# Late layer norms of the feed-forward stage: one step per gate and up block, several tiles under way, ln1 rows loaded once

## The chip, the cores and the metric

The kernel runs on one core of a Trainium2 chip. Its time is the device time of one execution in microseconds (us). The core has a matrix engine (PE in the profile, TensorE), three engines for elementwise work (DVE is VectorE, ACT is ScalarE, POOL is GpSimd) and a queue engine, SP, that here only issues DMAs. ACT also issues DMAs, for stores. Each engine works through its own instructions in order, and waits for the others by semaphores.

## The reference, cut to what matters

One layer of a network over 2048 latent tokens of width 1024: a mixer (attention beside a state-space branch, with a gated unit), then a feed-forward stage. The change lies at the seam of the two:

```python
x = layer_norm(DN_ALPHA * x + g1 * y_lat, lp['ln1_g'], lp['ln1_b'])
x = layer_norm(DN_ALPHA * x + g2 * swiglu(modulate(x, sh2, sc2), lp['w_gate_up'], lp['w_down']),
               lp['ln2_g'], lp['ln2_b'])

def modulate(x, shift, scale):
    return layer_norm(x) * (1 + scale) + shift
def swiglu(u, w_gate_up, w_down):
    gate, up = jnp.split(u @ w_gate_up, 2, axis=-1)
    return (jax.nn.silu(gate) * up) @ w_down
```

So between the mixer and the feed-forward each token passes two layer norms: one with the rows ln1_g and ln1_b (its result, x1, is also needed at the very end), one without, followed by shift and scale.

## The kernel before

All large products are fp32 in three passes: each operand is split into a high and a low part, and `mm3` (L63 to L65) multiplies high by high, low by high, high by low. A high part is a copy of the operand in fp32r (L53, on POOL for weights), a low part the difference (L58, mostly on DVE). So a weight tile that PE multiplies first passes POOL, then DVE.

The feed-forward class works on the tokens in two halves of 1024 (b = 0, 1), and in each on 22 blocks of 128 gate and 128 up columns (f = 0 to 21). A block is a 2 x 2 Strassen-Winograd scheme: seven products (0 to 6) of 12 matmuls, 84 in all, into the PSUM banks pa, pb, pc and pd (`block`). `weights(f + 1)` loads the next block's four weight pieces (tile wraw) and forms and splits their seven combinations (w0 to w3 and three g tiles) while block f is multiplied. Within a block DVE combines the banks: L1676, L1683, L1685, L1687, L1691. L1685 reads bank c, and product 6 goes on adding onto the same bank: PE can't begin product 6 (rows `pc<-oh,gh`) before DVE has done L1685. Product 0 of a block shows as `pa<-oh,w0h`.

The norms of the first 1024 tokens are done before the stage. Those of the second 1024 ("late" tiles 0 to 7, of 128 tokens each, held in n_scr) are done by `late(i)` beside the blocks of b = 0. The late tile i is started once every two blocks, all of it but the transposes at once: load n_scr and the four half rows of ln1_g and ln1_b (L1708, 256 KB each), norm (statistics L1714 and L1716 on DVE, square root and scale on ACT, L73 and L1721, and a few one-column operations on DVE between them), multiply and add the rows on POOL (L1727, L1728), store x1 (L1729, on ACT's queue), copy on DVE (L1732), norm again. Two blocks later the tile is transposed on PE (L1738, 8 transposes), shifted and scaled by ACT (L1741) and stored to u2_scr (L1743), from where `tokens(1)` loads it before b = 1. The tiles live in the pool ff_u (name uraw), 8 buffers; a tile's start takes eight of them (r, ln1_g, ln1_b, u2, two halves each).

No order is written out for this stage: the framework's scheduler lines up each engine's instructions by the order of the program text and its own estimates, so a change in the text shifts rows on every engine, also in the stages ahead.

Of the kernel before, what the change touches and what calls it, by code (L numbers as in the profile page):

```python
# [1541 lines left out]
class FeedForward:  # L1542
# [48 lines left out]
    def tokens(self, b):  # L1591

        nc, V = self.nc, self.nc.vector
        u = {n: [] for _, _, n in PRODUCTS}
        for k in range(4):
            t = {PRODUCTS[i][2]: self.pair() for i in STEP}
            r = {n: self.up.tile([128, 512], F32, name="uraw", bufs=8) for n in ("B11", "B12", "B21", "B22", "T1")}
            for n in ("B11", "B12", "B21", "B22"):
                j, h = int(n[1]) - 1, int(n[2]) - 1
                row, col = (j * 4 + k) * 128, (b * 2 + h) * 512  # L1600
                nc.sync.dma_start(r[n], self.E.u2_scr[row:row + 128, col:col + 512])

# [19 lines left out]
        return u  # L1622
# [34 lines left out]
    def block(self, b, f, w, u):  # L1657
# [35 lines left out]
        V.tensor_tensor(c22, c22, u2, ALU.mult)  # L1693
        self.store(b, f, 1, c22)

    def late(self, i):

        nc, E = self.nc, self.E
        V, P = nc.vector, nc.gpsimd
        t = NLAT // 128 - LATE + i  # L1700

        def piece():
            return self.up.tile([128, 512], F32, name="uraw", bufs=8)

        def load(src):
            p = [piece(), piece()]
            for h in range(2):
                nc.sync.dma_start(p[h], src(slice(h * 512, (h + 1) * 512)))  # L1708
            return p

        def norm(r):
            st = self.sm.tile([128, 2, 6], F32, name="lst", tag="lst", bufs=2)
            for h in range(2):
                V.bn_stats(st[:, h], r[h])  # L1714
            mv = self.sm.tile([128, 2], F32, name="bmv", tag="bmv")
            V.bn_aggr(mv, st)  # L1716
            rs = rsqrt(nc, self.sm, mv[:, 1:2], E.eps)
            nb = self.sm.tile([128, 1], F32, name="nb", tag="nb")
            V.tensor_scalar(nb, mv[:, 0:1], rs, -1.0, ALU.mult, ALU.mult)
            for h in range(2):  # L1720
                nc.scalar.activation(r[h], r[h], AF.Identity, bias=nb, scale=rs)  # L1721

        r = load(lambda h: E.n_scr[i, :, h])
        lg, lb = [load(lambda h: E.I[n][0:1, h].broadcast_to([128, 512])) for n in ("ln1_g", "ln1_b")]
        norm(r)
        for h in range(2):
            P.tensor_tensor(r[h], r[h], lg[h], ALU.mult)  # L1727
            P.tensor_tensor(r[h], r[h], lb[h], ALU.add)  # L1728
            nc.scalar.dma_start(E.x1_scr[t * 128:(t + 1) * 128, h * 512:(h + 1) * 512], r[h])  # L1729
        u2 = [piece(), piece()]  # L1730
        for h in range(2):
            V.tensor_copy(u2[h], r[h])  # L1732
        norm(u2)
        yield
        for h in range(2):
            pt = self.ps.tile([128, 512], F32, name="pd")
# [9 lines left out]
    def hidden(self, q, f):  # L1746

        t = self.pair()
        raw = self.up.tile([128, 512], F32, name="uraw", bufs=8)
# [62 lines left out]
    def run(self):  # L1812
        tc, nc, E, I = self.tc, self.nc, self.E, self.I
        with ExitStack() as st:
            self.tp = st.enter_context(tc.tile_pool(name="ff_t", bufs=8, side="right", reuse_waits="tile"))
            self.op = [st.enter_context(tc.tile_pool(name="ff_o%d" % k, bufs=7, side="right", reuse_waits="tile"))
                       for k in (3, 2, 1, 0)][::-1]
            self.up = st.enter_context(tc.tile_pool(name="ff_u", bufs=8, side="right", reuse_waits="tile"))
            self.rows = st.enter_context(tc.tile_pool(name="ff_r", bufs=1, reuse_waits="tile"))
            self.sm = st.enter_context(tc.tile_pool(name="ff_s", bufs=4, reuse_waits="tile"))  # L1820
            self.ps = st.enter_context(tc.tile_pool(name="ff_p", bufs=2, space=PSUM, reuse_waits="tile"))
            w = self.weights(0)
            u = self.tokens(0)
            late = iter(())
            for b in range(2):
                if b:
                    u = self.tokens(b)
                for f in range(NFB):
                    nxt = self.weights((f + 1) % NFB) if b == 0 or f + 1 < NFB else None
                    (self.block if b or f else self.first)(b, f, w, u)  # L1830
                    w = nxt
                    if b == 0 and f % 2:
                        next(late, None)
                        late = self.late(f // 2 - 1) if 0 <= f // 2 - 1 < LATE else iter(())
                        next(late, None)
            self.g2 = row_bcast(nc, self.rows, E.mod_scr[3:4, :], "g2b")
            self.lg = row_bcast(nc, self.rows, I["ln2_g"], "l2g")
            self.lb = row_bcast(nc, self.rows, I["ln2_b"], "l2b")
# [154 lines left out]
```

## Time and profile before

| | |
|---|---|
| median of 3 runs (lowest to highest) | 3283.35 us (3279.94 to 3284.1) |
| the profiled execution's own time | 3283.37 us |
| its span in the profile | 3281.6 us |
| PE busy | 3076.4 us, 94% of the span |
| DVE, POOL, ACT busy | 69%, 48%, 39% |
| gate and up blocks of b = 0 | about 1879 to 2350 us in the span |

The profiled execution lies 0.02 us from the median, so sums made against it hold for the runs as they are; 1.8 us of its time lie outside the span. A busy share is an average over the whole span; what an engine waits for is read in the stage in question.

### The profile page before, as it was taken

The numbers are of one execution on the slowest core, as the hardware profiler recorded it, in microseconds if no ns is written. First come the engines' busy times: TensorE is split into PE (matmuls) and PEld (weight loads), VectorE is DVE, ScalarE is ACT, GpSimd is POOL, SyncE is SP. The second block draws the span as 40 slices with busy tenths as digits, with TensorE's granted clock in tenths as the row PEclk, the third lists the DMA queues.
The fourth block names the chain that finished last, engine by engine and source line by source line (L and its number), as shares of the span: only waits on it lengthen the run. The fifth ranks groups of instructions, "written<-read, shape, count | busy, mean of one in ns | idle before, by whom it ended". The sixth has DMA issues, their size and how long they took to land. (4 is left out here: it accounts for less than half of the span.)

```text
span 3281.6 us, 48246 instructions
## 1 busy us (share of the span) xinstructions
PE 3076.4 (94%) x16693; PEld 2615.6 (80%) x16693; DVE 2272.8 (69%) x3938; ACT 1279.9 (39%) x2404; POOL 1581.2 (48%) x2365
## 2 busy tenths in 40 slices
PE   7899998999999999999789889889899999999998
PEld 4788877988988988888667677668688888888886
DVE  7755465888888776788477686666766666566667
ACT  2333354777777666667434233222201002112110
POOL 3755333877877899834243242332322222243444
PEclk9999999999999999999999999999899999999999
DMA  7444474111110222211768543343422224655544
GB/s 235 159 155 133 150 241 131 31 26 29 33 30 23 63 70 80 85 58 32 206 163 215 176 139 116 116 126 96 135 87 90 78 84 133 201 184 165 189 149 137
DMA packets 376885, 389.49 MB, mean 119 GB/s; under 512 B 97656, under 2 KB 270776, under 8 KB 376640
## 3 DMA queue, kind: packets, MB, share of 16 engines
q1 hardware_dynamic: 306640, 314.65, 32.3%
q10 hardware_dynamic: 70000, 71.75, 6.4%
q8 instruction: 132, 2.16, 0.3%
q14 instruction: 113, 0.93, 0.1%
HBM read 281.82 MB, written 104.48 MB: 118 GB/s over the span
## 5 line engine op out<-in xcount | busy, mean ns | idle before, releaser
L1033 DVE TENSOR_TENSOR ptl<-tps,pth 128x512 fp32r<-128x512 f32 x576 | 380.9, 685 | 100.3 <-ACT pth L1027 100.0
L1027 ACT CAST pth<-tps 128x512 fp32r<-128x512 f32 x576 | 335.9, 586 | 159.3 <-PE tps L1022 145.6
L53 POOL TENSOR_SCALAR gh<-wraw 128x512 fp32r<-128x512 f32 x220 | 178.4, 813 | 427.9 <-PE pc L64 97.2
L1045 PE MATMUL O<-pth,vhl 128*128 128x256 f32 x1152 | 322.9, 304 | 0.6 <-DVE oo L1054 0.6
L1046 PE MATMUL O<-ptl,vhl 128*128 128x256 f32 x1152 | 297.5, 282 | 2.0 <-DVE ptl L1033 1.8
L999 DVE TENSOR_REDUCE mx<-SB 128x1 f32<-128x1280 f32 x128 | 190.7, 1490 | 77.7 <-PE SB L65 77.7
L58 DVE TENSOR_TENSOR gl<-wraw,gh 128x512 fp32r<-128x512 f32 x216 | 166.5, 775 | 92.1 <-POOL gh L53 91.8
L1046 PEld LDWEIGHTS O<-ptl,vhl 128*128 128x128 f32 x1152 | 219.1, 190 | 10.0 <-DVE ptl L1033 3.4
L1045 PEld LDWEIGHTS O<-pth,vhl 128*128 128x128 f32 x1152 | 217.8, 189 | 7.6 <-ACT pth L1027 1.1
L1564 ACT CAST oh<-uraw 128x512 fp32r<-128x512 f32 x144 | 86.3, 620 | 319.8 <-PE pd L64 176.0
L1022 PE MATMUL tps<-ident,PB 128*128 128x128 f32 x1280 | 192.5, 272 | 4.6 <-DVE ptl L1033 4.6
L1010 ACT ACTIVATE PB<-SB,nm 128x1280 f32<-128x1280 f32 x128 | 170.7, 1333 | 4.2 <-DVE nm L1004 4.1
L1022 PEld LDWEIGHTS tps<-ident,PB 128*128 128x128 f32 x1280 | 152.2, 140 | 23.8 <-DVE ptl L1033 7.0
L999 DVE TENSOR_REDUCE mx<-SA 128x1 f32<-128x1024 f32 x128 | 156.1, 1219 | 17.7 <-PE SA L65 17.3
L1692 ACT ACTIVATE s<-s 128x512 f32<-128x512 f32 x43 | 27.1, 631 | 338.7 <-DVE s L1691 319.4
L1022 PE MATMUL tps<-ident,PA 128*128 128x128 f32 x1024 | 152.8, 274 | 1.1 <-DVE ptl L1033 1.1
L58 DVE TENSOR_TENSOR ol<-uraw,oh 128x512 fp32r<-128x512 f32 x136 | 104.4, 785 | 67.1 <-ACT oh L1564 66.9
L63 PE MATMUL SB<-kh,qh 96*128 96x512 f32 (+1 forms) x384 | 145.8, 380 | 0.0
L1010 ACT ACTIVATE PA<-SA,nm 128x1024 f32<-128x1024 f32 x128 | 143.5, 1121 | 5.3 <-DVE nm L1004 5.3
L774 POOL TENSOR_TENSOR sct<-scan_tab,hist 128x128 f32<-128x128 f32 x286 | 132.3, 463 | 24.5 <-ACT hist L763 4.9
L64 PE MATMUL SB<-kl,qh 96*128 96x512 f32 (+1 forms) x384 | 138.2, 360 | 0.0
L65 PE MATMUL SB<-kh,ql 96*128 96x512 f32 (+1 forms) x384 | 138.0, 359 | 0.0
(572 smaller groups left out, 9713.8 us busy)
## 6 DMA issues: line engine op xcount, KB each, us to landing
wraw<-in_w_down SPq DMA_DIRECT2D x198, 256.0 KB
wraw<-in_w_gate_up SPq DMA_DIRECT2D x176, 256.0 KB
h_scr<-s ACTq DMA_DIRECT2D x88, 256.0 KB
uraw<-h_scr SPq DMA_DIRECT2D x88, 256.0 KB
wad<-in_w_ada SPq DMA_DIRECT2D x32, 512.0 KB
wada<-in_w_ada SPq DMA_DIRECT2D x16, 512.0 KB
xt<-in_x SPq DMA_DIRECT2D x16, 512.0 KB
att_scr<-oo SPq DMA_DIRECT2D x64, 128.0 KB
```

Source lines behind the costliest of these rows:

```text
L53: eng.tensor_scalar(hi, raw, 1.0, 0.0, ALU.mult, ALU.add)
L58: eng.tensor_tensor(lo, raw, hi.bitcast(F32), ALU.subtract)
L63: nc.tensor.matmul(out, sh, mh, start=first, stop=False, skip_group_check=onto)
L64: nc.tensor.matmul(out, sh, ml, start=False, stop=False, skip_group_check=onto)
L65: return nc.tensor.matmul(out, sl, mh, start=False, stop=last, skip_group_check=onto)
L999: nc.vector.reduce_max(mx, SB if u else SA, axis=AX.X)
L1010: nc.scalar.activation(ex, SB if u else SA, AF.Exp, bias=hd.nm[:, u, t:t + 1], scale=SCALE, accum_out=hd.sums[:, u, t:t + 1])
L1022: nc.tensor.transpose(ps[:, kk, j * 128:(j + 1) * 128], pr.P[(j, u)][:, o:o + 128], ident)
L1027: nc.scalar.copy(hi, pr.pt[g][0])
L1033: nc.vector.tensor_tensor(lo, ps, hi.bitcast(F32), ALU.subtract)
L1045: nc.tensor.matmul(o, vk, hi[:, kk, :], start=k in (0, 8), stop=False)
L1046: nc.tensor.matmul(o, vk, lo[:, kk, :], start=False, stop=k in (7, 17))
```

## The change

`late(i)` becomes a generator of seven steps: load n_scr; statistics and square root; scale; multiply and add the rows on POOL and store x1; statistics and square root again; scale into u2; transposes and store. After every block of b = 0 each tile under way does one step; a tile begins every second block, from f = 0 on, so up to four are under way, and the last transposes follow block f = 20 where they followed f = 19. The rows ln1_g and ln1_b are loaded once, as two 512 KB tiles. The copy L1732 goes (the second scale writes to u2 itself), the one-column operations are written more tightly, the epsilon enters as ACT's bias. ff_u has 10 buffers, and the room for them comes from a smaller DMA scratch.

```diff
+    def piece(self):
+        return self.up.tile([128, 512], F32, name="uraw")
...
+        def stats(r):
+            st = sm.tile([128, 2, 6], F32, name="lst", tag="lst")
             for h in range(2):
                 V.bn_stats(st[:, h], r[h])
-            mv = self.sm.tile([128, 2], F32, name="bmv", tag="bmv")
+            mv = sm.tile([128, 2], F32, name="lmv", tag="lmv")
             V.bn_aggr(mv, st)
-            rs = rsqrt(nc, self.sm, mv[:, 1:2], E.eps)
...
+            sd = sm.tile([128, 1], F32, name="lsd", tag="lsd")
+            nc.scalar.activation(sd, mv[:, 1:2], AF.Sqrt, bias=E.eps)
+            return mv, sd
+
+        def scale(out, r, mv, sd):
+            a, b, nb = [sm.tile([128, 1], F32, name=n, tag=n) for n in ("lra", "lrb", "lnb")]
+            V.reciprocal(a, sd)
+            V.tensor_scalar(b, mv[:, 1:2], EPS, a, ALU.add, ALU.mult)
+            V.tensor_scalar(b, b, a, -0.5, ALU.mult, ALU.mult)
+            V.scalar_tensor_tensor(a, b, 1.5, a, ALU.add, ALU.mult)
+            V.tensor_scalar(nb, mv[:, 0:1], a, -1.0, ALU.mult, ALU.mult)
             for h in range(2):
-                nc.scalar.activation(r[h], r[h], AF.Identity, bias=nb, scale=rs)
...
-        lg, lb = [load(lambda h: E.I[n][0:1, h].broadcast_to([128, 512])) for n in ("ln1_g", "ln1_b")]
-        norm(r)
+                nc.scalar.activation(out[h], r[h], AF.Identity, bias=nb, scale=a)
+
+        r = [self.piece() for _ in range(2)]
         for h in range(2):
-            P.tensor_tensor(r[h], r[h], lg[h], ALU.mult)
-            P.tensor_tensor(r[h], r[h], lb[h], ALU.add)
...
+            nc.sync.dma_start(r[h], E.n_scr[i, :, halves[h]])
+        yield
+        m = stats(r)
+        yield
+        scale(r, r, *m)
+        yield
         for h in range(2):
-            V.tensor_copy(u2[h], r[h])
-        norm(u2)
+            P.tensor_tensor(r[h], r[h], self.l1g[:, halves[h]], ALU.mult)
+            P.tensor_tensor(r[h], r[h], self.l1b[:, halves[h]], ALU.add)
+            nc.scalar.dma_start(E.x1_scr[t * 128:(t + 1) * 128, halves[h]], r[h])
+        yield
+        m = stats(r)
+        yield
+        u2 = [self.piece() for _ in range(2)]
+        scale(u2, r, *m)
         yield
...
-            self.up = st.enter_context(tc.tile_pool(name="ff_u", bufs=8, side="right", reuse_waits="tile"))
+            self.up = st.enter_context(tc.tile_pool(name="ff_u", bufs=10, side="right", reuse_waits="tile"))
...
+            nc.sync.dma_start(self.l1g, I["ln1_g"].broadcast_to([128, D]))
+            nc.sync.dma_start(self.l1b, I["ln1_b"].broadcast_to([128, D]))
+            lates = []
...
-                    if b == 0 and f % 2:
-                        next(late, None)
-                        late = self.late(f // 2 - 1) if 0 <= f // 2 - 1 < LATE else iter(())
-                        next(late, None)
+                    if b == 0:
+                        if f % 2 == 0 and f // 2 < LATE:
+                            lates.append(self.late(f // 2))
+                        for l in lates:
+                            next(l, None)
```

In the new text the late statistics are L1709 and L1711, the square root L1713, the one-column operations L1718 to L1722, the scale L1724, the row operations on POOL L1735 and L1736, the x1 store L1737, the transposes L1747 and the u2_scr store L1752.

**DVE in a block of the later part of b = 0.** In a block that carries the start of a late tile, DVE's rows around L1685 were these before:

```order
L58 TENSOR_TENSOR w3l<-wraw,w3h 128x512 [waits PE_49,Pool_49]
L1732 COPY uraw<-uraw 128x512 [waits DMAHW1_49,DMAHW4_49,DMAHW0_49,Pool_49]
L1714 BN_STATS lst<-uraw 128x6 [waits DVE_49]
L1683 TENSOR_TENSOR s<-pb,d 128x512 [waits PE_49]
L58 TENSOR_TENSOR gl<-wraw,gh 128x512 [waits Pool_49]
L1685 TENSOR_TENSOR s<-pc,s 128x512 [waits DVE_49]
```

In such a block of the changed kernel they are these; it carries the first statistics of one tile and the second ones of the tile ahead (the numbers tell the buffers apart):

```order
L1709 BN_STATS lst_25157<-uraw_24989 128x6 [waits DMAHW6_49]
L1709 BN_STATS lst_25330<-uraw_24631 128x6
L58 TENSOR_TENSOR w3l_24284<-wraw_24295,w3h_24283 128x512 [waits PE_49,Pool_49]
L1709 BN_STATS lst_25157<-uraw_24990 128x6 [waits DMAHW7_49]
L1709 BN_STATS lst_25330<-uraw_24632 128x6
L1711 BN_AGGR lmv_25160<-lst_25157 128x2 [waits DVE_49]
L1711 BN_AGGR lmv_25333<-lst_25330 128x2 [waits DVE_49]
L1683 TENSOR_TENSOR s_24388<-pb_24319,d_24334 128x512 [waits DMAHW3_49,PE_49]
L58 TENSOR_TENSOR gl_24288<-wraw_24293,gh_24287 128x512 [waits Pool_49]
L1685 TENSOR_TENSOR s_24390<-pc_24320,s_24388 128x512 [waits DMAHW5_49,DVE_49]
```

The copy that waits for POOL's row operations is gone from ahead of L1683; four statistics rows, which wait for loads of earlier blocks, stand there instead, and the one-column operations that wait for ACT follow L1685.

**DVE in an early block.** In block f = 3 of the changed kernel DVE has these rows between L1676 and L1683, work of three tiles among them:

```order
L1709 BN_STATS lst_24614<-uraw_23915 128x6
L1709 BN_STATS lst_24614<-uraw_23916 128x6 [waits Pool_49]
L1711 BN_AGGR lmv_24617<-lst_24614 128x2 [waits DVE_49]
L58 TENSOR_TENSOR w2l_23598<-wraw_23610,w2h_23597 128x512 [waits DMAHW5_49,PE_49,Pool_49]
L1587 TENSOR_TENSOR wraw_23610<-wraw_23610,wraw_23607 128x512 [waits DVE_49]
L1709 BN_STATS lst_24799<-uraw_24631 128x6 [waits DMAHW4_49]
L1709 BN_STATS lst_24799<-uraw_24632 128x6 [waits DMAHW6_49]
L1718 RECIPROCAL lra_24621<-lsd_24446 128x1 [waits Activation_49]
L1711 BN_AGGR lmv_24802<-lst_24799 128x2 [waits DVE_49]
L58 TENSOR_TENSOR w3l_23600<-wraw_23611,w3h_23599 128x512 [waits PE_49,Pool_49]
L1719 TENSOR_SCALAR lrb_24622<-lmv_24444,lra_24621 128x1 [waits DVE_49]
L1718 RECIPROCAL lra_24783<-lsd_24619 128x1 [waits Activation_49]
```

Twelve more one-column operations follow, and only then L1683, gl and L1685: here waits for POOL's row operations and for ACT's square roots do stand ahead of L1685, where a block of before had one tile's copy. Block f = 2 is like it, with two tiles.

**SP at the gated unit, well ahead of the feed-forward stage.** SP's loads of the unit's input z stood behind the attention results (ab, awb) before:

```order
L1357 DMA ab<-att_scr 128x2x256 [waits DMAHW1_49,DVE_49]
L1360 DMA awb<-w_scr 64x2x256 [waits DMAHW3_49]
L1360 DMA awb<-w_scr 64x2x256 [waits DMAHW4_49]
L1252 DMA z<-z_scr 128x512 [waits DMAHW5_49]
L1252 DMA z<-z_scr 128x512 [waits DMAHW6_49]
```

In the changed kernel three of the four stand ahead of them, behind the load of an output weight (l1b), and the fourth stays behind:

```order
L1237 DMA l1b<-in_w_out 128x1024 [waits DMAHW6_49,PE_49]
L1055 DMA att_scr<-oo 64x2x256 [waits DMAHW0_49,DVE_49]
L1252 DMA z<-z_scr 128x512 [waits DMAHW1_49]
L1252 DMA z<-z_scr 128x512 [waits DMAHW2_49]
L1252 DMA z<-z_scr 128x512 [waits DMAHW3_49]
L1357 DMA ab<-att_scr 128x2x256 [waits DMAHW4_49,PE_49]
```

Nothing in the text of that stage is edited; the shift comes from the scheduler and from other addresses. On POOL the output weight's three operations move with it from behind the first four splits of z (zh) to ahead of them.

## Rows read from the trace of the kernel before

**Rows 1.** The page, part 1: busy us (share of span) x instructions.

```profile
PE 3076.4 (94%) x16693; PEld 2615.6 (80%) x16693; DVE 2272.8 (69%) x3938; ACT 1279.9 (39%) x2404; POOL 1581.2 (48%) x2365
```

**Rows 2.** Waits of PE from 1780 to 2420 us: total, times, longest.

```profile
PE pc L63 <- DVE s L1685: 39.0, 10, 6.1
PE pa L63 <- POOL w0h L53: 8.5, 1, 8.5
```

**Rows 3.** Timeline of PE, waits: start, duration, [idle before <- releaser].

```profile
1886.44 0.47 PE L63 MATMUL pb<-oh,w1h 128*128 128x512 f32 x1 [3.02 <-DVE s L1646]
...
1923.18 0.76 PE L63 MATMUL pc<-oh,gh 128*128 128x512 f32 x1 [3.01 <-DVE s L1685]
...
2015.93 0.77 PE L63 MATMUL pc<-oh,gh 128*128 128x512 f32 x1 [5.99 <-DVE s L1685]
...
2347.93 0.50 PE L63 MATMUL pc<-oh,gh 128*128 128x512 f32 x1 [1.79 <-DVE s L1685]
...
2392.50 0.50 PE L63 MATMUL pc<-oh,gh 128*128 128x512 f32 x1 [0.62 <-DVE s L1685]
```

**Rows 4.** Timeline of PE: the first matmul of four blocks.

```profile
1993.36 0.48 PE L63 MATMUL pa<-oh,w0h 128*128 128x512 f32 x1
...
2041.05 0.48 PE L63 MATMUL pa<-oh,w0h 128*128 128x512 f32 x1
...
2251.03 0.39 PE L63 MATMUL pa<-oh,w0h 128*128 128x512 f32 x1
...
2290.00 0.39 PE L63 MATMUL pa<-oh,w0h 128*128 128x512 f32 x1
```

**Rows 5.** Timeline from 2007 to 2015 us: SP, POOL, DVE.

```profile
2007.93 0.45 SPq L1708 DMA_DIRECT2D uraw<-in_ln_b  x1
...
2012.22 1.26 POOL L1728 TENSOR_TENSOR uraw<-uraw 128x512 f32<-128x512 f32 x1 [3.05 <-DMA uraw<-in_ln_b]
2013.45 1.20 POOL L53 TENSOR_SCALAR gh<-wraw 128x512 fp32r<-128x512 f32 x2
...
2014.10 1.08 DVE L58 TENSOR_TENSOR gl<-wraw,gh 128x512 fp32r<-128x512 f32 x1 [3.15 <-POOL gh L53]
```

**Rows 6.** Groups by form, 1880 to 2330 us: count | busy, mean ns | idle before.

```profile
L1728 POOL TENSOR_TENSOR uraw<-uraw 128x512 f32<-128x512 f32 x16 | 22.2, 1386 | 21.7 <-DMA uraw<-in_ln_b 21.5
...
L1714 DVE BATCH_NORM_STATS2 lst<-uraw 128x6 f32<-128x512 f32 x30 | 20.0, 675 | 0.2
...
L75 DVE RECIPROCAL rq_r<-rq_s 128x1 f32<-128x1 f32 x16 | 2.0, 153 | 0.2 <-ACT rq_s L73 0.2
```

**Rows 7.** Timeline of DVE and PE in a block without late work.

```profile
2262.66 0.69 DVE L58 TENSOR_TENSOR w3l<-wraw,w3h 128x512 fp32r<-128x512 f32 x1 [1.31 <-POOL w3h L53]
2264.83 0.69 DVE L1683 TENSOR_TENSOR s<-pb,d 128x512 f32<-128x512 f32 x1 [1.48 <-PE pb L65]
...
2266.03 0.69 DVE L1685 TENSOR_TENSOR s<-pc,s 128x512 f32<-128x512 f32 x1
...
2267.35 0.39 PE L63 MATMUL pc<-oh,gh 128*128 128x512 f32 x1
```

**Rows 8.** Timeline of POOL in block f = 2.

```profile
1907.17 1.70 POOL L1727 TENSOR_TENSOR uraw<-uraw 128x512 f32<-128x512 f32 x1 [0.29 <-ACT uraw L1721]
...
1914.42 1.04 POOL L53 TENSOR_SCALAR w3h<-wraw 128x512 fp32r<-128x512 f32 x1 [0.15 <-PE pc L64]
```

**Rows 9.** Windows: length, busy by engine (x), PEclk, DMA share, GB/s.

```profile
1880.00:1890.00 10.00, 6.98 (x32) 5.49 (x31) 9.87 (x16) 1.74 (x3) 2.75 (x4) 1.00 0.27 79
...
1920.00:1930.00 10.00, 6.99 (x19) 5.41 (x19) 9.45 (x20) 2.93 (x4) 6.41 (x5) 0.66 0.40 110
```

**Rows 10.** Timeline at the gated unit: SP, PE.

```profile
1573.88 0.50 SPq L1252 DMA_DIRECT2D z<-z_scr  x1
...
1584.19 2.07 PE L63 MATMUL pg<-zh,gh 128*128 128x512 f32 x4 [8.57 <-POOL zh L53]
```

**Rows 11.** Timeline of POOL where b = 1 begins.

```profile
2361.20 8.81 POOL L53 TENSOR_SCALAR w0h<-wraw 128x512 fp32r<-128x512 f32 x1 [14.80 <-PE pa L64]
```

More of the change, by code (lines that the diff above doesn't have):

```diff
@@ L1596, in tokens @@
             t = {PRODUCTS[i][2]: self.pair() for i in STEP}
-            r = {n: self.up.tile([128, 512], F32, name="uraw", bufs=8) for n in ("B11", "B12", "B21", "B22", "T1")}
+            r = {n: self.piece() for n in ("B11", "B12", "B21", "B22", "T1")}
             for n in ("B11", "B12", "B21", "B22"):
@@ L1694, in block @@
         self.store(b, f, 1, c22)
+    def piece(self):
+        return self.up.tile([128, 512], F32, name="uraw")
     def late(self, i):
-        nc, E = self.nc, self.E
+        nc, E, sm = self.nc, self.E, self.sm
         V, P = nc.vector, nc.gpsimd
         t = NLAT // 128 - LATE + i
[L1702 to L1709, printed above, removed]
@@ L1711, in norm @@
-        def norm(r):
-            st = self.sm.tile([128, 2, 6], F32, name="lst", tag="lst", bufs=2)
+        halves = [slice(0, 512), slice(512, 1024)]
+        def stats(r):
+            st = sm.tile([128, 2, 6], F32, name="lst", tag="lst")
             for h in range(2):
                 V.bn_stats(st[:, h], r[h])
-            mv = self.sm.tile([128, 2], F32, name="bmv", tag="bmv")
+            mv = sm.tile([128, 2], F32, name="lmv", tag="lmv")
             V.bn_aggr(mv, st)
-            rs = rsqrt(nc, self.sm, mv[:, 1:2], E.eps)
-            nb = self.sm.tile([128, 1], F32, name="nb", tag="nb")
-            V.tensor_scalar(nb, mv[:, 0:1], rs, -1.0, ALU.mult, ALU.mult)
+            sd = sm.tile([128, 1], F32, name="lsd", tag="lsd")
+            nc.scalar.activation(sd, mv[:, 1:2], AF.Sqrt, bias=E.eps)
+            return mv, sd
@@ L1723, in late @@
-        r = load(lambda h: E.n_scr[i, :, h])
-        lg, lb = [load(lambda h: E.I[n][0:1, h].broadcast_to([128, 512])) for n in ("ln1_g", "ln1_b")]
-        norm(r)
+                nc.scalar.activation(out[h], r[h], AF.Identity, bias=nb, scale=a)
+        r = [self.piece() for _ in range(2)]
         for h in range(2):
-            P.tensor_tensor(r[h], r[h], lg[h], ALU.mult)
-            P.tensor_tensor(r[h], r[h], lb[h], ALU.add)
-            nc.scalar.dma_start(E.x1_scr[t * 128:(t + 1) * 128, h * 512:(h + 1) * 512], r[h])
@@ L1730, in late @@
-        u2 = [piece(), piece()]
-        for h in range(2):
-            V.tensor_copy(u2[h], r[h])
-        norm(u2)
+            nc.sync.dma_start(r[h], E.n_scr[i, :, halves[h]])
[4 more added lines that the diff above has]
+        yield
+        for h in range(2):
+            P.tensor_tensor(r[h], r[h], self.l1g[:, halves[h]], ALU.mult)
+            P.tensor_tensor(r[h], r[h], self.l1b[:, halves[h]], ALU.add)
+            nc.scalar.dma_start(E.x1_scr[t * 128:(t + 1) * 128, halves[h]], r[h])
@@ L1748, in hidden @@
         t = self.pair()
-        raw = self.up.tile([128, 512], F32, name="uraw", bufs=8)
+        raw = self.piece()
         self.nc.sync.dma_start(raw, self.E.h_scr[f * 128:(f + 1) * 128, q * 512:(q + 1) * 512])
@@ L1821, in run @@
             self.ps = st.enter_context(tc.tile_pool(name="ff_p", bufs=2, space=PSUM, reuse_waits="tile"))
+            self.l1g = self.rows.tile([128, D], F32, name="l1g")
+            self.l1b = self.rows.tile([128, D], F32, name="l1b")
             w = self.weights(0)
             u = self.tokens(0)
-            late = iter(())
+            nc.sync.dma_start(self.l1g, I["ln1_g"].broadcast_to([128, D]))
+            nc.sync.dma_start(self.l1b, I["ln1_b"].broadcast_to([128, D]))
+            lates = []
             for b in range(2):
@@ L1982 @@
     a = layout(inputs)
-    nc = bacc.Bacc("TRN2", target_bir_lowering=False, num_devices=1)
+    nc = bacc.Bacc("TRN2", target_bir_lowering=False, num_devices=1, dynamic_dma_scratch_size=2048)
     arrays, ins = {}, {}
```

## The prediction

> **What bounds the kernel now.** The page first: PE is busy 94% of the span, DVE 69%, POOL 48% [rows 1]; so only what makes PE wait, or run slower, counts. The waits of PE in the feed-forward stretch come next. One row stands out: bank c waits for DVE's L1685 ten times, 39.0 us in all, with the longest at 6.1 [rows 2]. On the timeline two of the ten are after the late work, 1.79 and 0.62 us; the other eight fall while late tiles are under way [rows 3], so 39.0 - 1.79 - 0.62 = 36.6 us. One of the eight is 0.2 us (block f = 1), one 3.01 (f = 2), one about 4, the other five between 5.5 and 6.1, of which one is shown.
>
> A stall costs more than itself. [...] The block starts give the price. The pair of blocks with the 5.99 us stall lasts 2041.05 - 1993.36 = 47.69 us, a pair without one 2290.00 - 2251.03 = 38.97 [rows 4]. Both have eight transposes. The difference is 8.72 us, so 2.7 us are slow clock.
>
> Why L1685 is late is read backwards from 2015 us. DVE waits 3.15 us for a high part from POOL; POOL had waited 3.05 us for a half of ln1_b, which SP issued only at 2007.93 [rows 5]. The split of the weight stands behind the late tile's row operation on POOL, that one behind the load, the load behind a free uraw buffer. The groups say the same: 21.5 us of waiting for ln1_b loads ahead of L1728 alone [rows 6].
>
> **What the change removes.** The loads of ln1_g and ln1_b are no longer part of a tile, and neither the copy nor another wait for POOL stands ahead of L1685 in the later blocks. If the seven larger stalls and the small one go, with 2.7 us of slow clock behind each of the seven, that is 36.6 + 7 x 2.7 = 55.5 us. The fewer one-column operations, the 16 copies and the smaller DMA load are worth nothing beyond that, since DVE has idle time behind PE in such blocks (1.31 and 1.48 us in one place [rows 7]) and no wait for DMA is left in the chain.
>
> **The later blocks with late work, three of them.** Four statistics rows of 0.675 us [rows 6] and two small ones are 3.1 us of DVE work ahead of L1683. A block without late work leaves DVE 1.31 + 1.48 us idle there, more before, and L1685 ends (2266.03 + 0.69) 0.6 us before PE begins product 6 at 2267.35 [rows 7]. I expect the work to fit within a few tenths, and count 1.0 us for all later blocks. Bounds: 0, or 4 us each where a wait slips in.
>
> **The early blocks.** Here the scheduler has put two and three tiles into one block, and waits for POOL and ACT do stand ahead of L1685. I follow the rows by hand, with 1.35 us for a row operation (the mean of L1727 and L1728; L1728 alone 1.386 [rows 6]), 0.6 for a weight split [rows 5], 0.6 from start to start of DVE's full rows [rows 7], 0.1 to 0.2 for a one-column operation [rows 6].
> - f = 1: two more statistics rows on DVE, partly in idle time; the stall grows from 0.2 to 0.9 us.
> - f = 2: POOL began its row operations at 1907.17 and was at the split w3h by 1914.42 [rows 8]. Now, 0.7 us later, it does four for tile 0 (to 1913.3), two splits (1914.6), four for tile 1 (1920.0), then w3h (1920.7). DVE's w3l stands behind that (1921.4), then some ten one-column operations (1922.5), then L1683, gl and L1685 (1924.5). PE is ready at 1923.18 - 3.01 + 0.7 = 1920.9: a stall of 3.6, with slow clock 6.3 us. So this one is not removed.
> - f = 3: from its start at 1929.7, POOL alternates row operations and splits until 1939.7; DVE then has w2l, L1587, three tiles' small work and w3l (to 1946.0), and L1685 ends at 1947.9. Product 6 is due 16.3 us after the block's start ((2267.35 - 2251.03) [rows 4, 7]), at 1946.0: a stall of 1.9 us.
> - f = 4: ACT's copy L1673 is late behind x1 stores that wait for POOL; L1676 ends about 1.0 us after PE wants bank b.
>
> Whether a stall near 2 us costs slow clock as well the trace leaves open. One of 3.02 us, at 1886 us, left the granted clock at 1.00; one of 3.01 us, at 1923, has 0.66 in its window [rows 3, 9]. So I take half of 2.7 behind f = 3's. [...]
>
> The early blocks and the later ones together: 0.9 + 6.3 + (1.9 + 1.35) + 1.0 + 1.0 = 12.5 us stay. Bounds: 0 (the waits end sooner than I add up), and 25 (f = 1 to 4 each like a large stall of before, less the overlap).
>
> POOL and DVE run against each other there. POOL's row operations have taken up to 1.70 us [rows 8], and one split took 8.81 us at 2361 us instead of 0.6 [rows 11]. [...]
>
> **What moves elsewhere.** At the gated unit PE waits 8.57 us for the splits of z, whose loads SP issued at 1573.88, behind the attention results [rows 10]. Three of the four loads now come ahead, some 8 us sooner; but the output weight's operations (three on POOL, of 1024 columns each) stand ahead of the splits, and the fourth load is still behind. By hand the stall becomes 4 to 6 us in two pieces: 3 us gained. Bounds: 9 gained, 5 lost. The two loads of ln1_g and ln1_b are issued while PE works on the output projection, ahead of weights(1), and delay nothing: 0. (Without that cover they could hold weights(1) back by some 10 us, as long as it took from the issue of z at 1573.88 to PE's start [rows 10].) The last u2_scr store comes a block, 19 us, later, so tokens(1) begins about 7 us later within the last block; it then finds more of its loads issued at once (10 buffers for 8). PE waits there for a split once, 8.5 us [rows 2], because of the row of 8.81 [rows 11]. I take 0; bounds 8.5 either way.
>
> **Sum.** 3283.4 (the profiled execution's own time, 0.02 from the median) - 55.5 + 12.5 - 3 = 3237 us.
>
> **Rivals.**
> - The early blocks don't stall: tiles run ahead as the text has it, and waits on POOL and ACT end in time. Then 3283.4 - 55.5 - 3 = 3225. For it: DVE was idle for 5% of the time even at 1920 to 1930 us [rows 9], and a hand sum lines up waits that may overlap. Against it: the order of the rows in f = 2 and 3.
> - The stall only changes its releaser: statistics and one-column operations wait for ACT and POOL in the later blocks too. With 4 us in each of three later blocks and 25 early, 37 stay: 3283.4 - 55.5 + 37 - 3 = 3262. Against it: no row that waits for POOL or ACT stands ahead of L1685 in those.
> - No gain: the time freed comes back in full at the start of b = 1, because the second half of u2_scr is late and PE waits for it. It needs 52 us of idle PE there; the store is 19 us later at most, so hardly.
> - Slower: POOL starves. In blocks where DVE runs without a gap, a weight split of POOL takes 8 us, as at 2361 [rows 11], and PE waits 8.5 [rows 2] and has 2.7 of slow clock, 11.2 us. The sum gains 46 us, so it turns from the fifth such block on. With eight, one for each tile, 3237 + 90 = 3327. For it: the row exists, and two or three tiles at once make such stretches. Against it: at 1920 to 1930 us DVE was busy 9.45 of 10 us [rows 9] without such a row, and the split at 1914 took 1.04 [rows 8].
>
> **Chances and range.** Forecast (3230 to 3246) 0.48; early blocks free 0.22; stall in the later blocks 0.17; no gain 0.03; starved POOL, slower, 0.04; what I haven't seen, near the forecast or above, 0.06. The range for 8 in 10 reaches from 3216 (early blocks free, the z stall all gone) to 3262 (the second rival). A difference under 0.2%, 6.6 us, is about what a measurement of this kernel can't tell from none. Faster 0.92, same 0.03, slower 0.05.
>
> **What would show it.** Right: the waits of PE for L1685 fall from 39 us to about 10, the rest in f = 1 to 4; no wait of POOL for in_ln1 rows; blocks from f = 5 on at 19.1 or, with transposes, 19.9 us; a stall of z of 4 to 6 us. Wrong: waits for L1685 of 2 us or more beyond f = 5 (second rival), none at all (first), splits of POOL over 3 us (starving), or a wait of more than 10 us where b = 1 begins.

## The result, and the profile after

| | before | changed |
|---|---|---|
| median (lowest to highest) | 3281.64 us (3272.42 to 3284.1) | 3239.89 us (3237.78 to 3241.2) |
| the profiled execution's own time | 3283.37 us | 3237.78 us |
| its span | 3281.6 us | 3235.9 us |

The ratio is 0.9877, with a 95% interval of 0.9857 to 0.9898: faster, by 1.2%. The total lies 3 us from the forecast of 3237, but the terms of the sum missed by more than that, and cancelled. Some of it is luck: the same kernel measured again (run 11) has 3249.91 us, 13 above the forecast. The page of the changed kernel has this first line (busy us, share, instructions; [rows 1]):

```profile
PE 3064.9 (95%) x16693; PEld 2602.4 (80%) x16693; DVE 2260.4 (70%) x3906; ACT 1275.6 (39%) x2400; POOL 1573.3 (49%) x2365
```

The waits of PE from 1780 to 2420 us, to be held against [rows 2] (total, times, longest):

```profile
PE pc L63 <- DVE s L1685: 11.6, 4, 6.2
```

L1685 has gone from 39.0 us to 11.6; the text gave about 10. Two of the four waits, 2.0 us, lie behind the late tiles, as two did before. The timeline of PE in the same kernel shows where they are (start, duration, idle before and its releaser; rows without a bracket are block starts), to be held against [rows 3, 4]:

```profile
1849.82 0.47 PE L63 MATMUL pa<-oh,w0h 128*128 128x512 f32 x1 [1.41 <-DVE xo L1438]
...
1879.75 0.66 PE L63 MATMUL pb<-oh,w1h 128*128 128x512 f32 x1 [3.13 <-DVE s L1646]
...
1892.21 0.50 PE L63 MATMUL pb<-oh,gh 128*128 128x512 f32 x1 [0.84 <-DVE s L1676]
...
1920.74 0.77 PE L63 MATMUL pc<-oh,gh 128*128 128x512 f32 x1 [6.23 <-DVE s L1685]
...
1925.20 0.39 PE L63 MATMUL pa<-oh,w0h 128*128 128x512 f32 x1
...
1945.06 0.77 PE L63 MATMUL pc<-oh,gh 128*128 128x512 f32 x1 [3.35 <-DVE s L1685]
...
1949.33 0.39 PE L63 MATMUL pa<-oh,w0h 128*128 128x512 f32 x1
...
1957.88 0.47 PE L63 MATMUL pa<-oh,w2h 128*128 128x512 f32 x1 [2.95 <-ACT d L1673]
...
1973.19 0.39 PE L63 MATMUL pa<-oh,w0h 128*128 128x512 f32 x1
...
2109.47 0.39 PE L63 MATMUL pa<-oh,w0h 128*128 128x512 f32 x1
...
2126.51 0.47 PE L63 MATMUL pc<-oh,gh 128*128 128x512 f32 x1 [0.56 <-POOL gh L53]
...
2130.16 0.48 PE L63 MATMUL pa<-oh,w0h 128*128 128x512 f32 x1
...
2286.08 0.48 PE L63 MATMUL pa<-oh,w0h 128*128 128x512 f32 x1
...
2358.07 0.39 PE L63 MATMUL pa<-oh,w0h 128*128 128x512 f32 x1
```

Behind f = 0 (whose 3.13 us were 3.02 before) three waits above 2 us are left, in blocks f = 2, 3 and 4 (the latter two from 1925.20 and 1949.33 us). From f = 5 (1973.19) to f = 20 no block waits for L1685; the worst of them, f = 12, takes 2130.16 - 2109.47 = 20.69 us, 0.85 over the 19.84 of a quiet one (one without a wait) with transposes; a quiet one without transposes takes 19.04 to 19.17. Where the time came from, by stages that begin and end at the same matmul in both traces:

| stage, begin to begin of | before | after | difference |
|---|---|---|---|
| program start to block f = 0 | 1855.77 | 1849.82 | -5.95 |
| f = 0 to f = 21, the late tiles | 473.20 | 436.26 | -36.94 |
| f = 21 to b = 1's f = 2 | 76.36 | 71.99 | -4.37 |
| from there to the end of the span | 876.27 | 877.83 | +1.56 |

They add up to the span's -45.7. The second line splits once more: up to the start of f = 5 the changed kernel is 5.63 us slower than before (1973.19 - 1849.82 = 123.37 for 1973.51 - 1855.77 = 117.74), from there to f = 21 it is 42.57 faster (312.89 for 355.46). Of the 5.63 us, 1.7 are slow clock behind the wait of f = 0: the first matmul behind it takes 0.66 us, 0.47 before [rows 3], and its product lasts 4.41 us (to 1884.16) where others take 2.72. The granted clock over that product is 0.61; before it was 1.00 from 1886.44 to 1890 us. Why the clock fell there and not before is not shown.

### The profile page after: what moved, and what is told of

Its sections match the earlier page's. It is cut to its first block, busy times and chain, and to the rows that moved or that the text cites. A ratio compares the mean times of both kernels' runs of the same rounds, so it can differ in the third digit from the quotient of the medians.

```text
span 3235.9 us, 48094 instructions
## 1 busy us (share of the span) xinstructions
PE 3064.9 (95%) x16693; PEld 2602.4 (80%) x16693; DVE 2260.4 (70%) x3906; ACT 1275.6 (39%) x2400; POOL 1573.3 (49%) x2365
## 5 line engine op out<-in xcount | busy, mean ns | idle before, releaser
L1692 ACT ACTIVATE s<-s 128x512 f32<-128x512 f32 x43 | 27.1, 631 | 286.1 <-DVE s L1691 286.0
```

## The experiments

Each time is a median, each ratio (with its 95% interval) that to the kernel before on the same chip.

**1. The smaller DMA scratch alone.**

```diff
-num_devices=1)
+num_devices=1, dynamic_dma_scratch_size=2048)
```

> The kernel before with the smaller DMA scratch (2048) alone; nothing of the late tiles is edited. Theory: the shift at the gated unit comes from other addresses, not from the late tiles. Then z's splits stall PE for about 5.6 and 1.2 us where they stalled it for 8.57, the feed-forward stage begins about 5 to 6 us earlier than before (near 1850 us), the ten waits for L1685 stay at about 39 us, and the time is 3276 to 3280. Rival: the shift follows from the new text of the late tiles; then the time is that of before, 3282 to 3284, with the 8.57 us stall in place.

3278.46 us, ratio 0.9985 (0.9974 to 0.9995), in the theory's range. L1685's waits stay, and yet the feed-forward stage begins 7.15 us earlier than before, at 1848.62. The two views are the waits of PE from 1780 to 2420 us and its timeline:

```profile
PE pc L63 <- DVE s L1685: 38.9, 10, 6.3
```

```profile
1588.76 1.65 PE L63 MATMUL pg<-zh,gh 128*128 128x512 f32 x3 [6.52 <-POOL zh L53]
...
1597.73 0.49 PE L63 MATMUL pg<-zh,gh 128*128 128x512 f32 x1 [1.63 <-POOL zh L53]
...
1848.62 0.47 PE L63 MATMUL pa<-oh,w0h 128*128 128x512 f32 x1 [1.41 <-DVE xo L1438]
```

So the gain ahead of the feed-forward stage belongs to the scratch, a number that the change sets too, and not to the late tiles. Its size differs from program to program: the thirteen profiles with the smaller scratch begin the stage 2.6 to 9.6 us before the kernel before. How the scratch does it is not shown. z's wait itself shrinks little (8.15 us in two pieces for 8.57, where the theory had 5.6 and 1.2); the two waits for gsg behind it, 2.47 and 0.84 us where before there were 4.50 and 3.01, give more.

**2. The rows loaded once, each tile still in one go.** The scratch of run 1, and the rows l1g, l1b allocated and loaded as in the change:

```diff
-        lg, lb = [load(lambda h: E.I[n][0:1, h].broadcast_to([128, 512])) for n in ("ln1_g", "ln1_b")]
...
-            P.tensor_tensor(r[h], r[h], lg[h], ALU.mult)
-            P.tensor_tensor(r[h], r[h], lb[h], ALU.add)
+            P.tensor_tensor(r[h], r[h], self.l1g[:, h * 512:(h + 1) * 512], ALU.mult)
+            P.tensor_tensor(r[h], r[h], self.l1b[:, h * 512:(h + 1) * 512], ALU.add)
```

> The kernel before with ln1_g and ln1_b loaded once (and the smaller scratch, without which there is no room); each tile still does all but its transposes at once, copies included, and uraw keeps 8 buffers. Theory (the late loads are the cause): the waits for L1685 fall from 39 us to 8 to 14, blocks from f = 5 on take 19.1 to 19.9 us, and the time is 3230 to 3242, as with the full change. Rival (a whole tile in one block is the cause: DVE's copies and one-column operations wait there for POOL and ACT): six blocks keep stalls of 2 to 5 us, the waits stay above 20 us, and the time is 3250 to 3272.

3248.63 us, ratio 0.9892 (0.9877 to 0.9908): between the two ranges. The waits of PE from 1780 to 2420 us say why:

```profile
PE pa L63 <- ACT d L1673: 10.3, 5, 2.5
PE pc L63 <- DVE s L1685: 9.9, 4, 3.6
```

L1685 falls as the theory has it, and a wait that was not there before comes up in f = 7, 9, 11 and 13: bank a isn't copied in time. ACT's timeline ahead of one of them, and then DVE's:

```profile
2008.00 0.34 ACTq L1728 DMA_DIRECT2D x_scr<-uraw  x1
2009.56 0.33 ACTq L1626 DMA_DIRECT2D h_scr<-s  x1
2009.92 1.28 ACT L1692 ACT_TABLE_LOAD   x1 [7.43 <-DMA x_scr<-uraw]
...
2011.75 0.57 ACT L1673 COPY d<-pa 128x512 f32<-128x512 f32 x1
```

```profile
2006.75 1.76 DVE L58 TENSOR_TENSOR gl<-wraw,gh 128x512 fp32r<-128x512 f32 x1 [2.42 <-POOL gh L53]
2008.44 1.09 DVE L1688 TENSOR_TENSOR s<-s 128x512 f32<-128x512 f32 x1
```

ACT's queue holds the x1 stores, which wait for POOL's row operations, then the store of the block before to h_scr, the activation L1692 and the copy. What ends last is not an x1 store, the last of which is issued at 2008.00, but DVE's L1688, whose result the h_scr store takes: it ends at 2009.53, behind a split gl that waited 2.42 us for POOL's gh. POOL's row operations hold both. Three of the four blocks take 24.2 us, 4.3 above a quiet one with transposes, and one 22.5.

**3. The rows loaded for each tile, into buffers of their own.**

```diff
...
-            p = [piece(), piece()]
+            p = p or [piece(), piece()]
...
-        lg, lb = [load(lambda h: E.I[n][0:1, h].broadcast_to([128, 512])) for n in ("ln1_g", "ln1_b")]
+        lg, lb = [load(lambda h: E.I[n][0:1, h].broadcast_to([128, 512]), [self.up.tile([128, 512], F32, name="lrow", bufs=4) for _ in range(2)]) for n in ("ln1_g", "ln1_b")]
```

> The kernel before with the rows ln1_g and ln1_b still loaded for each tile, but into four buffers of their own instead of uraw's (and the smaller scratch). Theory (the load waits for a uraw buffer, not the transfer or its issue): as with rows loaded once, within 5 us, waits for L1685 8 to 14 us. Rival (the four loads per tile cost by themselves, on SP's queue or in flight): POOL still waits 2 to 3 us for in_ln1 rows in each of six blocks, and the time stays above 3255.

3257.58 us, ratio 0.9919 (0.9904 to 0.9935). POOL no longer waits for in_ln1 rows at all (35.7 us from 1880 to 2330 before), though all 32 loads are still made, so the rival's mechanism is out, though the time lies in its range: the wait was for a uraw buffer. It is 9 us above run 2 where 5 were allowed, and L1685 keeps 15.7 us in six waits, the longest 6.9 in f = 3, where the tiles fall in another order. That block takes 29.43 us for 19.81 in run 2, which is the 9 us: the row operations of a second tile fall into it, and DVE's copy L1732, ahead of L1683 and L1685, waits 4.00 us for them. What remains has run 2's form, five waits for L1673, 10.3 us.

**4. A tile's load held until its block.**

```diff
         for h in range(2):
+            nc.scalar.copy(r[h][:, 0:1], after[:, 0:1])
             nc.sync.dma_start(r[h], E.n_scr[i, :, halves[h]])
```

Here `after` is the block's gate tile g1, which `block` now returns.

> The changed kernel, but the load of a tile's n_scr also waits for the gate of the block that it is put behind (a one-column ACT copy into each half of the buffer ahead of the load), so that tiles can't run ahead. Theory (what stays of the stalls comes from five tiles piled up in blocks f = 1 to 4): no wait of PE over 2 us in f = 2 to 4, these three blocks at 19 to 20 us each instead of about 28, 24.1 and 23.9, and the time is 3220 to 3228. Rival (each tile costs the same wherever it lies): the stalls come back as 1 to 2 us in each of eight blocks, and the time is 3234 to 3244.

3247.37 us, ratio 0.9889 (0.9875 to 0.9904): the rival's form and a little more than its price. In f = 2 and 3 waits of 1.1 and 3.0 us stay, and every later pair of blocks with a tile has one of 0.8 to 1.0 us for L1686 (L1685 in its line numbers) and, but for the first, one of 1.1 to 1.3 us for bank a: 41.7 us for 39.0. A tile whose whole chain runs in one block isn't free.

**5. The first scale held until the block's first copy.** Loads and first statistics run ahead; `end` is d, the copy of bank a.

```diff
+            if end is not None:
+                nc.scalar.copy(nb, end[:, 0:1])
             V.tensor_scalar(nb, mv[:, 0:1], a, -1.0, ALU.mult, ALU.mult)
```

> The changed kernel, with the first scale of each tile held until bank a has been copied in the block behind which that step stands in the text (a one-column ACT copy ahead of L1722, the last one-column operation); loads and first statistics may still run ahead. So each second block, from f = 2 on, carries one tile's row operations, and POOL begins them some 4 us into it, as in the undisturbed block f = 10 of the changed kernel (2113.78 us in a block from 2109.47). Theory (what stays is five tiles piled up in f = 2 to 4): those three blocks lose their 8.0, 5.0 and 4.0 us, no wait of PE is above 1.5 us there, and the time is 3221 to 3230. Rival (a tile whose steps follow each other at once costs 2 to 3 us wherever it lies, as where only the load was held: 41.7 us a pair of blocks for 39.0): 3242 to 3252.

(The block from 2109.47 us, which the expectation calls f = 10, is f = 12.) 3252.95 us, ratio 0.9908 (0.9891 to 0.9926): the rival again, 1 us above its range. Eight blocks wait 1.8 to 3.1 us for L1686, and DVE's timeline in one of them shows statistics that wait for POOL ahead of the split w2l:

```profile
1995.53 1.29 DVE L1711 BATCH_NORM_STATS2 lst<-uraw 128x6 f32<-128x512 f32 x2 [2.56 <-POOL uraw L1740]
...
1998.75 1.06 DVE L58 TENSOR_TENSOR w2l<-wraw,w2h 128x512 fp32r<-128x512 f32 x1
```

**6. No row operations on POOL.** The 32 multiplications and additions are left out, as the expectation says.

```diff
-            P.tensor_tensor(r[h], r[h], self.l1g[:, halves[h]], ALU.mult)
-            P.tensor_tensor(r[h], r[h], self.l1b[:, halves[h]], ALU.add)
```

> The changed kernel without the 32 row operations on POOL (the multiplication by ln1_g and the addition of ln1_b are left out of the second 1024 tokens); all else as it is, five tiles still run ahead. Theory (POOL's chain of row operations ahead of w3h sets L1685 in f = 2 and 3, and holds the x1 stores ahead of L1673 in f = 4): the waits of 6.2, 3.35 and 2.95 us fall below 1.5, 0.5 and 0.5, and the time is 3222 to 3230. Rival (DVE's own statistics and one-column rows of five tiles hold L1685): over 2 us stay in f = 2 and over 1 us in f = 3, and the time is 3232 to 3240.

3222.72 us, ratio 0.9822 (0.9803 to 0.984): the theory. The waits of PE from 1900 to 2280 us are one row:

```profile
PE pc L63 <- DVE s L1685: 1.1, 1, 1.1
```

All statistics and one-column rows of the five piled-up tiles are still there, and cost 1.1 us. What the early blocks of the changed kernel lose, they lose to POOL's row operations and what queues behind them. In f = 3 1.06 us stay where 0.5 were given.

**7. The steps, with the rows loaded for each tile into uraw.**

```diff
...
+        lg, lb = [[self.piece() for _ in range(2)] for _ in range(2)]
+        for p, n in ((lg, "ln1_g"), (lb, "ln1_b")):
+            for h in range(2):
+                nc.sync.dma_start(p[h], E.I[n][0:1, halves[h]].broadcast_to([128, 512]))
         scale(r, r, *m)
...
```

POOL's row operations read lg and lb, and the two 512 KB loads are gone.

> The changed kernel with ln1_g and ln1_b again loaded for each tile into uraw's ten buffers, one step ahead of the row operations. Theory (the loads that wait for uraw buffers are the cause, steps or not): POOL again waits for in_ln1 rows in most blocks with late work, PE waits of 2 to 6 us follow, and the time is 3255 to 3275. Rival (the seven steps are what counts, since the loads then come early enough): no such wait beyond f = 5, and the time is 3236 to 3248.

3257.71 us, ratio 0.9924 (0.9908 to 0.9941): the theory. POOL waits 14.6 us for in_ln1 rows, PE 23.2 us for L1685, 2.2 to 3.2 us of it in each of four blocks beyond f = 5.

**8. Ten uraw buffers for the kernel before** (and the scratch).

```diff
-name="uraw", bufs=8
+name="uraw", bufs=10
```

> The kernel before with ten uraw buffers for eight (and the smaller scratch), late tiles and their loads as before. Theory on the start of b = 1 (its 8.5 us wait for w0h goes because the token loads find ten buffers): that wait falls below 2 us, and this alone gives some 5 us. Rival (it goes because the late tiles end earlier or later): the wait of 8.5 us stays. Theory on the late tiles (loads wait for a free buffer): two more buffers shorten but don't remove the waits for L1685, 20 to 35 us of 39 stay; time 3250 to 3274, against 3278 with the smaller scratch alone.

3275.71 us, ratio 0.9973 (0.9962 to 0.9984), just above the range. L1685 keeps 34.6 us, POOL's waits for in_ln1 rows 25.3; the wait of 8.55 us where b = 1 begins stays, so ten buffers are not what removed it.

**9, 10 and 11. The scale held by earlier rows, and the changed kernel again.** As run 5, with `end` the tile c22 of the block before (9) or its u3 (10).

```diff
-        return s1
+        return c22        # 10: return u3; both handed to the step one block later
```

> As the run with the first scale held, but held only by the last product of the block before (c22 of block f + 1, for the step that stands behind block f + 2). Nothing else differs; on POOL the four row operations now stand two ahead of the split w1h and two behind it, as in block f = 10 of the changed kernel, where they stood all four behind w1h. Theory (the 2.4 us per tile there came from four row operations in a row ahead of the split w2h, on which w3l, L1684 and so L1686 wait): the waits for L1686 fall from 1.8 to 2.4 us to under 0.7 in each block with row operations, a pair of blocks takes 39.0 to 39.9 us in place of 41.7, and the time is 3222 to 3232. Rival (DVE's second statistics and one-column rows in the same block cost 2 us wherever POOL's rows stand): 41 us or more a pair, 3244 to 3254.

> The same, held by a still earlier row of the block before (u3 of block f + 1, written by L1688 while its last product runs). On POOL two row operations then stand ahead of the split w0h and two behind it, all four ahead of w1h. Theory (the earlier the row operations are out of the way of w2h, the less DVE waits): no wait for L1686 above 0.3 us in those blocks, 39.0 to 39.4 us a pair, and the time is 3220 to 3229. Rival (row operations ahead of w0h and w1h only move the wait to those splits): waits of 1 to 3 us for w1h, w0h or bank a, 3234 to 3250.

> The changed kernel once more, unaltered, beside the two others: its time on the same chip is what they are to be held against. Every theory: a ratio to the kernel before within 0.985 to 0.990, 3233 to 3246.

Run 9: 3256.22 us, ratio 0.9918 (0.9905 to 0.9931). The theory fails: on POOL the row operations do stand two and two about w1h, and L1686 still waits 2.4 to 3.1 us in six of the eight blocks. Run 10: 3234.57 us, ratio 0.985 (0.9835 to 0.9864): 1.95 us in f = 2, 1.08 in each of the next five such blocks, pairs of 40.3 to 40.4 (the first, without transposes, 39.4). That is 1.3 to 1.9 us less waiting a tile than in run 9, a time in the rival's range without the rival's waits, and not the theory's 0.3. Run 11: 3249.91 us, ratio 0.9896 (0.9882 to 0.9911), in its range of ratios and above its range of times. It is the same program as the changed kernel, 10 us apart; the two profiled executions differ by 5.5 us, of which 2.7 lie at the start of b = 1 (below) and 2.2 in f = 0 to f = 21. Its interval overlaps that of the first comparison; run 10's, on the same chip, lies below it.

A hint stands in the last two tiles: they wait 1.0 and 1.1 us in run 9 for 2.4 to 3.1, and not at all in run 10. Beside them no further tile has its first statistics. In the other blocks of run 9 DVE does two statistics of one tile, two of the next and the one-column rows of both between L1677 and L1684, and the split w1l takes 1.76 us beside a row operation of POOL (at 1994.65), where the split gl takes 0.69 with POOL idle (at 1987.22). Run 12 takes that apart.

**12. The first statistics held too.**

```diff
+            if end is not None:
+                for h in range(2):
+                    nc.scalar.copy(st[:, h, 0:1], end[:, 0:1])
```

> As the run held by u3, and a tile's first statistics are held too, by u3 of the block before the step's own (a one-column ACT copy into each half of lst ahead of L1714). The block with POOL's row operations then has no statistics and no one-column rows on DVE; both tiles' statistics stand at the seam to the next block, their one-column rows ahead of the split w2l there. Theory (what is left of the wait, 1.08 us a tile, is DVE's rows of two tiles between L1677 and L1684 in the block in which POOL's row operations stretch them): no wait for L1686 above 0.4 us in those blocks, 38.9 to 39.5 us a pair, ratio to the kernel before 0.981 to 0.984. Rival (the rows only move: four statistics in a row now delay L1677 or w1l, and PE waits for bank b): 1 to 2 us of waits for L1677 in every second block, ratio 0.985 to 0.989.

3226.43 us, ratio 0.9843 (0.983 to 0.9856). From f = 3 on no block waits any more. The waits of PE from 1900 to 2280 us are one row, in f = 2, and its timeline gives 19.04 us a block and 19.86 with transposes:

```profile
PE pc L63 <- DVE s L1686: 1.1, 1, 1.1
```

```profile
1918.74 0.47 PE L63 MATMUL pc<-oh,gh 128*128 128x512 f32 x1 [1.13 <-DVE s L1686]
...
1921.58 0.39 PE L63 MATMUL pa<-oh,w0h 128*128 128x512 f32 x1
...
1940.62 0.39 PE L63 MATMUL pa<-oh,w0h 128*128 128x512 f32 x1
...
1978.70 0.39 PE L63 MATMUL pa<-oh,w0h 128*128 128x512 f32 x1
...
1998.56 0.48 PE L63 MATMUL pa<-oh,w0h 128*128 128x512 f32 x1
```

The rival's wait for L1677 isn't there. The ratio is 0.0003 above the theory's range: the late tiles are all but free now, and a wait outside their stage is as it was in run 11 (4.72 us at the start of b = 1, below). This version beats the kernel before and, by interval, both comparisons of the changed one; beside run 10 the intervals overlap.

## Why the prediction was right, point by point

**The cause.** Right. POOL's waits for in_ln1 rows are gone, L1685 with them, and runs 2, 3 and 7 take the parts apart: rows loaded once, or into buffers of their own, end the waits for loads; the steps without that don't (7). Rows loaded once give most of the gain, 3248.63 us. What the steps add is not shown: run 2's ratio of 0.9892 lies beside the changed kernel's 0.9877 and 0.9896. They remove the waits for L1673 that run 2 has in later blocks, and pay with the pile in the early ones.

**The 55.5 us removed.** About right. f = 0 to f = 21 gained 36.94, and what stays (next) comes to about 20, so some 57 went, or 59 with the slow clock of f = 0.

**The 12.5 us that stay.** Mis-sized: about 20. The text gave f = 1 0.9, f = 2 6.3, f = 3 3.25, f = 4 1.0 and the later blocks 1.0. Measured: f = 1 0.84 (but at bank b, for L1676; bank c has no wait there); f = 2 6.23 of waiting and 1.74 of slow clock (product 6 behind the wait lasts 1925.20 - 1920.74 = 4.46 us, at a granted clock of 0.61, and one of the seven products of a quiet block of 19.04 lasts 2.72), 8.0 in all; f = 3 24.13 - 19.04 = 5.1; f = 4 23.86 - 19.04 = 4.8; later 1.2. The common cause, POOL's row operations, was as told. That f = 1 fits is luck: its wait is the remainder of another, which the text didn't count. Before:

```profile
1897.84 0.50 PE L63 MATMUL pb<-oh,gh 128*128 128x512 f32 x1 [1.41 <-DVE s L1676]
```

In f = 2 the step that failed is the duration of a row operation, 1.35 us. POOL's timeline there:

```profile
1901.14 1.29 POOL L1735 TENSOR_TENSOR uraw<-uraw,l1g 128x512 f32<-128x512 f32 x1
...
1914.50 1.26 POOL L1736 TENSOR_TENSOR uraw<-uraw,l1b 128x512 f32<-128x512 f32 x1
1915.73 0.62 POOL L53 TENSOR_SCALAR w3h<-wraw 128x512 fp32r<-128x512 f32 x1
```

The eight take 12.4 us, 1.55 each, and w3h ends 1.6 us later than worked out once the 5.95 us shift of the whole stage is taken off; the rest of the 2.6 us is a split w3l of 1.06 us and a PE that was ready 0.4 us sooner. So the eight, of 1.26 to 1.74 us each, lost 1.6 against a mean that held long rows already, one of 1.70 [rows 8] among them. f = 4 missed most, 4.8 us for 1.0. The text had the x1 stores hold L1673, and so L1676 late by 1.0 us at bank b, product 4. The wait came two products earlier, where product 2 needs bank a itself, 2.95 us. ACT's timeline shows the stores, and DVE's what they share the delay with:

```profile
1947.16 7.60 ACTq L1737 DMA_DIRECT2D x_scr<-uraw  x4
1954.98 0.33 ACTq L1626 DMA_DIRECT2D h_scr<-s  x1
1955.34 1.28 ACT L1692 ACT_TABLE_LOAD   x1 [10.80 <-DVE s L1688]
...
1957.17 0.57 ACT L1673 COPY d<-pa 128x512 f32<-128x512 f32 x1
```

```profile
1951.48 1.77 DVE L58 TENSOR_TENSOR gl<-wraw,gh 128x512 fp32r<-128x512 f32 x1 [3.04 <-POOL gh L53]
```

The x1 stores are out at 1954.76; the h_scr store behind them still waits 0.2 us for DVE's L1688, which follows that split and ends at 1954.94. Both hang on POOL's row operations, so the stores alone are not the cause.

Run 6 shows that POOL's row operations stand behind the waits of f = 2, 3 and 4. Whether f = 3's wait costs slow clock was left open, and half of 2.7 us taken; its block says 5.09 - 3.35 = 1.74, and the first matmul behind the wait takes 0.77. All three waits cost 1.7 to 1.9 us in this way, where [rows 4] had 2.7 for a block and its neighbour. The granted clock was 0.61, 0.64 and 0.59 behind them (1920.74 to 1925.20, 1945.06 to 1949.33 and 1957.88 to 1960.60 us). In the kernel before it was 0.50 behind the wait of 5.99 us, 0.93 over the pair of blocks with that wait and 1.00 over the pair without one (windows, columns as in [rows 9]):

```profile
1993.36:2041.05 47.69, 41.70 (x179) 34.06 (x178) 29.77 (x57) 12.32 (x22) 15.29 (x19) 0.93 0.40 121
2015.93:2020.00 4.07, 4.07 (x10) 3.20 (x11) 3.79 (x7) 0.00 (x0) 0.00 (x0) 0.50 0.42 120
2251.03:2290.00 38.97, 38.97 (x177) 32.36 (x176) 23.62 (x37) 6.42 (x14) 10.33 (x14) 1.00 0.31 95
```

**The gated unit, 3 us.** Too small: 5.95 us by the start of the feed-forward stage, 1.0 of which was there before the unit. z's wait shrank from 8.57 to 5.63 + 1.17, by 1.8, less than the 3 that the text gave it; the waits for gsg and others behind it, which the text left out, gave the rest.

```profile
1588.11 1.65 PE L63 MATMUL pg<-zh,gh 128*128 128x512 f32 x3 [5.63 <-POOL zh L53]
```

**The start of b = 1, 0 us.** Off by 4.4, within its bounds. Run 11 is the same program, and there PE waits 4.73 us for w3h in that place, 0.53 in the first profile; the stage takes 74.70 us for 71.99 and for 76.36 before. So 2.7 of the 4.4 us are chance. The first profile is the rarer case: seven of the nine profiles with the steps have a wait for w3h of 2.9 to 4.7 us there; it and run 6's don't. The wait of 8.5 us for w0h stands in the profiles of before and of runs 1, 2, 3 and 8, where a tile is done in one go, and in none with the steps; why is not shown.

**The later blocks, 1.0 us.** Right (1.2), and so was the first part of what would show it: three tiles, at 2035, 2074 and 2113 us, with no wait of PE above 0.56.

## What to carry to other kernels

Here a queue in order made a late load cost what stood behind it on the next engine: four loads for rows that never change, waiting for working buffers, held weight splits and so PE, 39.0 us at L1685, and loading them once (9.9 us, run 2) gave most of the gain. Work that fits into idle time only does so if it is kept apart: a generator that yields between steps doesn't pace anything when a scheduler may move its steps ahead, and the row operations of five tiles ran between 1901 and 1955 us, in f = 2, 3 and the start of f = 4; a one-column copy from a tile of the block made the order hold. Where two engines slow each other (in the changed kernel a row operation of POOL took 1.26 to 1.28 us with no full sum or split of DVE beside it and up to 1.74 with one, and a split of DVE 0.69 alone and up to 1.78 beside a row operation), put the work of the first where the second has the least else to do, as run 12 did.

## What the runs showed of the hardware

**A weight split of POOL took 6.17 us beside a run of DVE rows, and 0.75 in another execution of the program.** The prediction left the 8.81 us split [rows 11] open. Two profiles of the same program show it with and without. In run 11, the timeline of POOL, then PE, then DVE:

```profile
2328.31 6.17 POOL L53 TENSOR_SCALAR w2h<-wraw 128x512 fp32r<-128x512 f32 x1 [3.88 <-issue]
2334.45 0.61 POOL L53 TENSOR_SCALAR w3h<-wraw 128x512 fp32r<-128x512 f32 x1
```

```profile
2335.12 0.79 PE L63 MATMUL pc<-oh,w3h 128*128 128x512 f32 x1 [4.73 <-POOL w3h L53]
```

```profile
2329.10 0.68 DVE L1578 TENSOR_TENSOR wraw<-wraw 128x512 f32<-128x512 f32 x1
...
2333.32 0.68 DVE L1583 TENSOR_TENSOR wraw<-wraw 128x512 f32<-128x512 f32 x1
2334.51 1.08 DVE L58 TENSOR_TENSOR w2l<-wraw,w2h 128x512 fp32r<-128x512 f32 x1 [0.51 <-POOL w2h L53]
```

The split, by its record, begins inside a run of DVE rows of two SBUF inputs that follow each other every 0.6 us, and ends 0.5 us behind the last. In the first profile of the changed kernel the same split takes 0.75 us, and a DVE row is the one that is stretched:

```profile
2325.78 0.75 POOL L53 TENSOR_SCALAR w2h<-wraw 128x512 fp32r<-128x512 f32 x1 [3.88 <-issue]
```

```profile
2325.97 1.09 DVE L1615 TENSOR_TENSOR uraw<-uraw 128x512 f32<-128x512 f32 x1
```

In the first case nine DVE rows, none of them stretched (0.68 us each), ran between the beginning and the end of one split; in the second one DVE row took 1.09 us and the split 0.75. What decides between the two is not shown. PE's wait of 4.73 us comes from the long split, in one execution of a program and not in another.

**DVE's rows are stretched only in some forms.** In block f = 12 of the changed kernel, DVE and then POOL:

```profile
2114.07 1.66 DVE L1583 TENSOR_TENSOR wraw<-wraw 128x512 f32<-128x512 f32 x1
...
2117.53 0.67 DVE L1676 TENSOR_TENSOR s<-pb,d 128x512 f32<-128x512 f32 x1
```

```profile
2113.78 1.41 POOL L1735 TENSOR_TENSOR uraw<-uraw,l1g 128x512 f32<-128x512 f32 x1 [0.88 <-ACT uraw L1724]
2115.26 1.62 POOL L1736 TENSOR_TENSOR uraw<-uraw,l1b 128x512 f32<-128x512 f32 x1
...
2117.44 1.29 POOL L1735 TENSOR_TENSOR uraw<-uraw,l1g 128x512 f32<-128x512 f32 x1
```

L1583, of two SBUF tiles, takes 1.66 us across two row operations of 1.41 and 1.62; L1676, which reads a PSUM bank and one SBUF tile, takes 0.67 beside a row operation of 1.29. The shortest rows of the two kinds in this kernel are 0.64 and 1.26 us. The same shows beyond this block. Between 1880 and 2330 us of the profiles of before and of the changed kernel, 8 full rows with a PSUM input begin inside a row operation of POOL and take 0.67 to 0.68 us; of 31 sums, differences and products of two SBUF tiles that do so, 29 take 1.10 to 1.79, and two, which begin in the last 0.05 us of one, take 0.67 and 0.68.
